# A hybrid backbone layer: raw weight buffers taken in turn, one head's filling, modulation's closing products, and four adds on GpSimd

## The chip, the core and the metric

The kernel runs on one core of a Trainium2 chip. The time is the device time of one execution in microseconds (us); for a kernel it is the median of several runs. TensorE (PE) does the matrix products, VectorE (DVE), ScalarE (ACT) and GpSimd (POOL) the elementwise work, and SyncE (SP) issues all the transfers spoken of here, in one queue, in order: a transfer whose wait isn't over holds back those behind it.

## The reference

One layer (DEPTH = 1) over x (1024 tokens x 1024) with 256 context tokens. Cut to what matters:

```python
mod = silu(c) @ w_mod + b_mod
sh1, sc1, ga1, sh2, sc2, ga2 = split(mod, 6)          # six chunks of 1024
hx = rmsnorm(x, g_mix) * (1 + sc1) + sh1
y = mlstm_mixer(hx, hc, w_in, b_gate, head_gain, w_out)   # 4 heads, two directions
x = x + ga1 * y
hx = rmsnorm(x, g_ffn) * (1 + sc2) + sh2
gate, val = split(hx @ w_up, 2)                       # w_up: 1024 x (2 * 2816)
x = x + ga2 * ((silu(col_conv3(gate) + b_conv) * val) @ w_down)
return rmsnorm(x, g_final)
```

Everything is float32 to the outside. The kernel makes one such product of three products of split numbers (high and low part), so one logical product of a 128x128 block is three PE instructions.

## The kernel before, in words

**The mixer.** It runs head by head. `mlstm(h)` is a generator: first the backward state over ten chunks of 128 tokens, then for each of eight token tiles i `scores(i + 2)` (products s, then the weights on DVE and ACT), `values(i)` (the numerators nm on PE, then dn, ha on DVE and ACT) and `readout(i - 1)` (the transposes yp on PE, which read ha). In the last head `readout` writes yh and yl, the split output, straight to the tiles that the out-projection reads. Each `yield` of `mlstm` carries a number, and `weave(main, fill)` adds these up and runs one unit of the filler for each whole one, and what is left of the filler behind the head. The numbers in the part over the token tiles are multiples of `pace` (1; in the last head 0.8). In heads 0 to 2 the filler is the projections of the next head (pv, pk, pq), in the last head `first_pair`: the out-projection of the first two heads, 16 units of twelve products opa (128x512) behind some loads and splits. What follows the last head, `second_pair`, begins with the products opb, which read the last head's yh and yl.

**Modulation beside it.** `along` runs one unit of `mods` after each unit of the filler in heads 0 to 2. `mods` are four sums one after the other (chunks 3, 4, 2 and 5 of w_mod): `mod_sum` loads eight raw tiles, adds each to ga (L658, `acc`) on DVE, and closes with `use(acc)`: for `mod_cols` eight tiny products mcp (L665, 128x2), for `mod_bcast` two products mbp (L676), which read ga.

**The channel mixer.** 22 tiles of 128 columns, ff, each with seven products in the manner of Strassen (p1 to p7), and each of these twelve PE instructions of 128x512: 84 for an ff. The weights of one ff are two raw tiles of 512 KB, rg (gate) and rv (value). `prep_gate` splits rg into ag (high part on ACT, low part on DVE: the names end in h and l). `prep_rest` makes with four adds on DVE the combinations sa and sb (two buffers for both), splits sb into at and sa into as, and then half of rv into av. p1 and p2 read ag, p6 and p5 read as, p3 and p7 read at, p4 reads av. On the other side stand the split activations ba, bs, bt, bu, made once before ff 0 in four k-tiles (their adds partly on GpSimd, L1016). `gate0` adds e and p2 into gt, `finish_gate` and `finish_value` make e, gt, t; t goes to memory (actd). From ff 11 on `act_sums` reads an earlier actd back (sr), makes sw and writes both (sums). `first(ff)` of ff 0 to 3, and with it p1 and p2, runs ahead of the loop (`pre`).

**Buffers and order.** Raw tiles have two buffers under the tag raw and one under raw2 (`raw_tile`). In the channel mixer rg takes raw, rv always raw2, so that rv of an ff can be loaded when av of the ff before has been split. `pp`, the PSUM tiles of the products, has eight buffers. The order of the instructions on each engine is fixed when the program is built: a scheduler sorts them by their dependences, the buffers and the order in which the code issues them; `tc.issue_after(i)` makes it put an instruction behind another.

Of the kernel before, what the change touches and what calls it, by code (L numbers as in the profile page):

```python
# [12 lines left out]
ALU = mybir.AluOpType  # L13
# [3 lines left out]
P = 128  # L17
# [7 lines left out]
H = 4  # L25
DK = 128
DV = 256
DFF = 2816
# [11 lines left out]
def backbone(ctx, tc, x, c, ctxt, c_ctx, w_mod, b_mod, g_mix, g_ffn, w_in, b_gate,  # L40
             head_gain, w_out, w_up, w_conv, b_conv, w_down, g_final, out):
    nc = tc.nc
    V, S, T, G = nc.vector, nc.scalar, nc.tensor, nc.gpsimd
# [6 lines left out]
    w_up = w_up[0]  # L50
    w_down = w_down[0]
    out = out[0]
# [10 lines left out]
    def wtile(name, dt=F32R, n=1024):  # L63
        return wp.tile([P, WT], dt, tag="w", bufs=8, name=name)[:, :n]

    def raw_tile(name, n=1024, other=False):
        tag, b = ("raw2", 1) if other else ("raw", 2)
        return wp.tile([P, WT], F32, tag=tag, bufs=b, name=name)[:, :n]

    def load_raw(src, name, other=False):  # L70

        r = raw_tile(name, other=other)
        nc.sync.dma_start(out=r if len(src.shape) == 2 else r.rearrange("p (a b) -> p a b", a=src.shape[1]), in_=src)
        return r

    def split(raw, name):

        n = raw.shape[1]
        hi = wtile(name + "h", n=n)
        lo = wtile(name + "l", n=n)  # L80
        S.copy(hi, raw)
        V.tensor_tensor(out=lo, in0=raw, in1=hi.bitcast(F32), op=ALU.subtract)
        return hi, lo
# [6 lines left out]
    def kp(src):  # L90
        return src.rearrange("(k p) n -> p k n", p=P)
# [159 lines left out]
    for i in range(16):  # L251
# [3 lines left out]
                    in1=bmc[:, 0:16].unsqueeze(2).to_broadcast([P, 16, 2]), op=ALU.add)  # L255
    V.scalar_tensor_tensor(out=smod, in0=mts[:, 8:16, :], scalar=1.0,
                           in1=gmix.unsqueeze(2).to_broadcast([P, KT, 2]), op0=ALU.add, op1=ALU.mult)
# [230 lines left out]
    def mlstm(h):  # L488
# [69 lines left out]
        def scores(i):  # L558
            ch = i + 2
            jb = NCH + 1 - ch  # L560
            f0, b0 = h * NCH + ch, H * NCH + h * NCH + jb
            sl = slice(i * P, (i + 1) * P)
            sp_ = st(f"s{h}_{i}")
            T.matmul(sp_[:, :P], kT[:, ch * P:(ch + 1) * P], qT[:, sl], start=True, stop=True)
            if i < LCH - 1:
                ktrans(ch, sp_, P)
                kscale(0, ch, sp_, P)

            ee = hp.tile([P, 2, P], F32, tag="ee", bufs=2, name=f"ee{h}_{i}")
            wi = hp.tile([P, 2, P], F32, tag="wi", bufs=3, name=f"wi{h}_{i}")  # L570
            if i % 2 == 0:
                mrows(i // 2)
            for d, (cc, pos) in enumerate(((f0, i), (b0, jb - 2))):
                mrow_ = mb[d, pos // 2][:, pos % 2, :]
                V.scalar_tensor_tensor(out=ee[:, d, :], in0=mrow_, scalar=uco[:, cc:cc + 1],
                                       in1=zmask[:, d, :], op0=ALU.subtract, op1=ALU.max)
                S.activation(out=wi[:, d, :], in_=mrow_, func=AF.Exp, scale=-1.0,  # L577
                             bias=mpco[:, cc:cc + 1])
            S.activation(out=ee, in_=ee, func=AF.Exp, scale=-1.0)
            V.tensor_tensor(out=ee, in0=ee, in1=sp_[:, :P].unsqueeze(1).to_broadcast([P, 2, P]), op=ALU.mult)  # L580
            wh = hp.tile([P, 2, P], F32R, tag="wh", bufs=3, name=f"wh{h}_{i}")
            wl = hp.tile([P, 2, P], F32R, tag="wl", bufs=3, name=f"wl{h}_{i}")
            S.copy(wh, ee)
            V.tensor_tensor(out=wl, in0=ee, in1=wh.bitcast(F32), op=ALU.subtract)
            V.tensor_tensor(out=wi, in0=wi, in1=qT[:, sl].unsqueeze(1).to_broadcast([P, 2, P]), op=ALU.mult)
            ws[i] = wh, wl, wi, f0, b0, jb
# [27 lines left out]
        def readout(i):  # L614
            sl = slice(i * P, (i + 1) * P)
            ha = hs.pop(i)
            yp = st(f"yp{h}_{i}")
            for f in range(2):
                T.transpose(yp[:, f * P:(f + 1) * P], ha[:, f * P:(f + 1) * P], ident)
            if h < H - 1:  # L620
                yt = hp.tile([P, 2, P], F32, tag="yt", bufs=2, name=f"yt{h}_{i}")
                for f in range(2):
                    S.mul(yt[:, f, :], yp[:, f * P:(f + 1) * P], hgain[:, 2 * h + f:2 * h + f + 1])
                nc.sync.dma_start(out=ydram[h][:, :, sl].rearrange("f p t -> p f t"), in_=yt)
            else:
                for f in range(2):
                    yh, yl = yhl[h][f]
                    gcol = hgain[:, 2 * h + f:2 * h + f + 1]
                    S.mul(yh[:, sl], yp[:, f * P:(f + 1) * P], gcol)
                    V.scalar_tensor_tensor(out=yl[:, sl], in0=yp[:, f * P:(f + 1) * P], scalar=gcol,  # L630
                                           in1=yh[:, sl].bitcast(F32), op0=ALU.mult, op1=ALU.subtract)

        pace = 1 if h < H - 1 else 0.8
        scores(0)
        yield pace
        scores(1)
# [8 lines left out]
        yield pace  # L645
        readout(LCH - 1)

    def mod_sum(chunk, name, use, acc):

        V.memset(acc, 0.0)  # L650
        nc.sync.dma_start(out=acc[0:1, :], in_=b_mod[:, chunk * D:(chunk + 1) * D])
        for k in range(KT):
            r_ = load_raw(w_mod[k * P:(k + 1) * P, chunk * D:(chunk + 1) * D], f"{name}r{k}", True)
            yield
            yield
            dve = next(i for i in reversed(nc.cur_bb.bb.instructions) if i.engine == mybir.EngineType.DVE)
            with tc.issue_after(dve):
                V.scalar_tensor_tensor(out=acc, in0=r_, scalar=sct[:, k, 0:1], in1=acc, op0=ALU.mult, op1=ALU.add)  # L658
        use(acc)

    def mod_cols(dst, gain=None):
        def use(acc):
# [53 lines left out]
    def along(units, side):  # L716

        for i, _ in enumerate(units):
            if i > 2:
                next(side, None)  # L720
            yield

    mods = chain(mod_sum(3, "m3", mod_cols(h2col), ga2), mod_sum(4, "m4", mod_cols(s2col, gffn), ga2),
                 mod_sum(2, "m2", mod_bcast(ga1), ga1), mod_sum(5, "m5", mod_bcast(ga2), ga2))
    EARLY = 6
    late = iter(())
# [127 lines left out]
    def split_to(hi, lo, src):  # L854
        S.copy(hi, src)
        V.tensor_tensor(out=lo, in0=src, in1=hi.bitcast(F32), op=ALU.subtract)
# [12 lines left out]
        trans2(0, tt - 4)  # L869
        split_to(ba[tt - 4][0], ba[tt - 4][1], bs[0, tt - 4])  # L870

    def add(out_, a_, b_, op=ALU.add):
        V.tensor_tensor(out=out_, in0=a_, in1=b_, op=op)  # L873

    def b_op(i, kt):

# [6 lines left out]

    aw = {}

    def load_up(ff, off, name, other=False):
        return load_raw(kp(w_up[:, off + ff * P:off + (ff + 1) * P]), f"{name}{ff}", other)

    def prep_gate(ff, raw=None):

        h_, l_ = split(raw if raw is not None else load_up(ff, 0, "rg"), f"ag{ff}")
        aw[ff, 1] = h_[:, :512], l_[:, :512]
        aw[ff, 2] = h_[:, 512:], l_[:, 512:]
# [16 lines left out]
    second_pair(range(4), 1, norm2)  # L910
    second_pair(range(4, 8), 0, first_half)
    rg0 = load_up(0, 0, "rg")
    prep_gate(0, rg0)
    second_pair(range(4, 8), 1, norm2)
# [15 lines left out]
    def split_b(i, kt, src):  # L930
        split_to(*b_op(i, kt), src)

    def prep_rest(ff, rg):

        rv = load_up(ff, DFF, "rv", True)
        sa, sb = [pc.tile([P, 1024], F32, tag="sx", bufs=2, name=f"{n}{ff}") for n in ("sa", "sb")]
        a11, a12, a21, a22 = rg[:, :512], rg[:, 512:], rv[:, :512], rv[:, 512:]
        add(sa[:, :512], a21, a22)
        add(sa[:, 512:], sa[:, :512], a11, ALU.subtract)
        add(sb[:, :512], a11, a21, ALU.subtract)  # L940
        add(sb[:, 512:], a12, sa[:, 512:], ALU.subtract)
        h_, l_ = split(sb, f"at{ff}")
        aw[ff, 7], aw[ff, 3] = (h_[:, :512], l_[:, :512]), (h_[:, 512:], l_[:, 512:])
        yield
        h_, l_ = split(sa, f"as{ff}")
        aw[ff, 5], aw[ff, 6] = (h_[:, :512], l_[:, :512]), (h_[:, 512:], l_[:, 512:])
        yield
        w_ = wtile(f"av{ff}")
        split_to(w_[:, :512], w_[:, 512:], a22)
        aw[ff, 4] = w_[:, :512], w_[:, 512:]  # L950
# [7 lines left out]
    def first(ff, pq=None):  # L958
        p1, p2 = pq or products(ff, (1, 2))
        e1 = u2k(f"e{ff}")  # L960
        S.copy(e1, p1)
        return e1, p2
# [45 lines left out]

    PRE = 4
    rest0 = prep_rest(0, rg0)  # L1010
    next(rest0)
    pre = [first(0), first(1)]
# [24 lines left out]
    def prep_next(ff):  # L1037

        rg = load_up(ff, 0, "rg")
        res = None  # L1040
        if ff >= PRE:
            prep_gate(ff, rg)
            res = first(ff)
        for _ in prep_rest(ff, rg):
            pass
        return res or pre[ff]

# [204 lines left out]
```

## Time and profile before

| | us |
|---|---|
| median of 3 runs | 1230.25 (1229.15 to 1230.99) |
| the profiled execution | 1229.65 |
| its span | 1227.9 |
| PE busy in the span | 1188.6 (97%) |
| DVE busy | 887.0 (72%) |
| ACT busy | 508.0 (41%) |
| GpSimd busy | 58.6 (5%) |

The span is what the profiler recorded of that execution, from the first to the last instruction. A busy time counts the time in which an instruction of the engine runs; PE's products overlap, so one of 0.39 us begins each 0.227 us. "Idle before" is the time in which the engine had nothing running, with the event that ended it. The granted clock of PE is given as a share of full speed.

The mixer ends at 520 us, the out-projection and the second norm to 576, the channel mixer's up part from 576 to 1008 (ff 16 starts at 887), then the down part.

### The profile page before, as it was taken

What the parts mean: (1) busy time and instruction counts of PE and PEld (TensorE: products, weight loads), DVE (VectorE), ACT (ScalarE), POOL (GpSimd) and SP (SyncE); (2) the same over time, 40 slices, a digit from 0 to 9 for tenths busy, and PEclk for the clock granted to TensorE, in tenths of its full rate; (3) what the DMA queues carried; (4) which work ended last, traced back from release to release, by engine and by line L of the source; (5) the groups of instructions that cost most, each with busy time, mean ns of one, the idle gap of its engine ahead of it and who ended that gap; (6) DMA issues with size and microseconds to landing.
All of it is one profiled execution on the core that took longest, in us unless ns stands there. A gap on an engine that the chain in (4) does not pass through costs nothing.

```text
span 1227.9 us, 15991 instructions
## 1 busy us (share of the span) xinstructions
PE 1188.6 (97%) x5811; PEld 978.5 (80%) x5811; DVE 887.0 (72%) x1564; ACT 508.0 (41%) x911; POOL 58.6 (5%) x198
## 2 busy tenths in 40 slices
PE   7999999999999999899999999999999999999996
PEld 1788998888888788787777888888877778888885
DVE  3775664566477558636998877788788877985887
ACT  3853353344355435327543342333333344444452
POOL 0100010001001001002000000000000000000011
PEclk9999999999999999999999999999999999999998
DMA  8622243343244342132233223244444459624523
GB/s 322 215 70 62 85 127 95 95 138 104 65 146 155 124 144 77 31 124 104 69 103 103 86 69 103 85 139 144 165 154 155 165 200 398 229 95 151 177 69 120
DMA packets 121248, 161.45 MB, mean 131 GB/s; under 512 B 8140, under 2 KB 83148, under 8 KB 121168
## 3 DMA queue, kind: packets, MB, share of 16 engines
q1 hardware_dynamic: 121168, 160.42, 38.9%
q8 instruction: 46, 0.75, 0.3%
q14 instruction: 34, 0.28, 0.1%
HBM read 125.75 MB, written 34.64 MB: 131 GB/s over the span
## 4 chain that ended last, share of the span: by engine, by line
PE 31%; DVE 13%; DMA 4%; ACT 3%; issue 2%; POOL 0%; DVEq 0%; POOLq 0%; ACTq 0%
PE p L87 5%; PE p L88 5%; PE p L86 5%; DMA rv<-in_f_w_up_dram 4%; PE pa L87 3%; PE pa L86 3%; PE pa L88 3%; PE pb L88 2%; PE pb L87 2%; PE pb L86 2%; DVE sb L873 1%; DVE gt L873 1%; DVE t L977 1%; DVE t L979 1%; DVE sa L873 1%
## 5 line engine op out<-in xcount | busy, mean ns | idle before, releaser
L873 DVE TENSOR_TENSOR gt<-e,p 128x512 f32<-128x512 f32 x66 | 44.9, 682 | 5.7 <-PE p L88 5.6
L611 DVE SCALAR_TENSOR_TENSOR ha<-ha,hms,so 128x256 f32<-128x256 f32 x32 | 15.5, 485 | 44.1 <-POOL hms L126 44.1
L873 DVE TENSOR_TENSOR e<-e,p 128x512 f32<-128x512 f32 x66 | 45.0, 681 | 1.3 <-PE p L88 0.9
L976 ACT ACTIVATE t<-gt,cols 128x1024 f32<-128x1024 f32 x22 | 27.4, 1245 | 42.8 <-DVE gt L873 42.8
L982 ACT ACTIVATE t<-t 128x1024 f32<-128x1024 f32 x22 | 23.4, 1062 | 48.1 <-DVE t L979 48.1
L977 DVE SCALAR_TENSOR_TENSOR t<-gt,cols,t 128x960 f32<-128x960 f32 x22 | 26.8, 1217 | 19.7 <-ACT t L976 19.7
L341 ACT CAST vh<-pv 128x256 fp32r<-128x256 f32 x30 | 11.1, 371 | 60.1 <-PE pv L88 60.1
L86 PE MATMUL p<-bt,av 128*128 128x512 f32 x88 | 34.2, 389 | 0.0
L87 PE MATMUL p<-bt,av 128*128 128x512 f32 x88 | 34.2, 389 | 0.0
L88 PE MATMUL p<-bt,av 128*128 128x512 f32 x88 | 34.2, 389 | 0.0
L125 POOL TENSOR_SCALAR fms<-fms 128x1 f32<-128x1 f32 x8 | 3.8, 472 | 628.2 <-DVE fms L873 628.2
L86 PE MATMUL nm<-vh,wh 128*128 128x258 f32 x64 | 31.0, 484 | 0.0
L342 DVE TENSOR_TENSOR vl<-pv,vh 128x256 fp32r<-128x256 f32 x30 | 12.7, 423 | 24.9 <-ACT vh L341 24.9
L604 ACT ACTIVATE ha<-nm,dn 128x256 f32<-128x256 f32 x32 | 15.1, 473 | 32.6 <-DVE dn L602 31.2
L577 ACT ACTIVATE wi<-mb,bco 128x128 f32<-128x128 f32 x64 | 22.6, 399 | 12.6 <-PE nm L594 8.0
L979 DVE SCALAR_TENSOR_TENSOR t<-gt,cols,t 128x960 f32<-128x960 f32 x22 | 26.7, 1212 | 0.0
L873 DVE TENSOR_TENSOR sa<-rv 128x512 f32<-128x512 f32 x22 | 15.2, 689 | 15.3 <-DMA rv<-in_f_w_up_dram 15.3
L86 PE MATMUL pk<-hx,wk_0h 128*128 128x512 f32 x64 | 25.3, 395 | 0.0
L88 PE MATMUL pq<-hx,wq_0h 128*128 128x512 f32 x64 | 25.1, 393 | 0.0
L86 PE MATMUL pq<-hx,wq_0h 128*128 128x512 f32 x64 | 25.1, 393 | 0.0
L87 PE MATMUL pk<-hx,wk_0l 128*128 128x512 f32 x64 | 25.0, 391 | 0.0
L88 PE MATMUL pk<-hx,wk_0h 128*128 128x512 f32 x64 | 25.0, 390 | 0.0
(1096 smaller groups left out, 4169.8 us busy)
## 6 DMA issues: line engine op xcount, KB each, us to landing
rg<-in_f_w_up_dram SPq DMA_DIRECT2D x25, 512.0 KB, 3.9
rv<-in_f_w_up_dram SPq DMA_DIRECT2D x22, 512.0 KB, 4.6
actd<-t SPq DMA_DIRECT2D x22, 512.0 KB, 2.8
dr<-in_f_w_down_dram SPq DMA_DIRECT2D x44, 256.0 KB, 5.2
dr<-sums SPq DMA_DIRECT2D x44, 256.0 KB, 2.9
dr<-actd SPq DMA_DIRECT2D x33, 256.0 KB, 5.1
mr<-in_w_mod_dram SPq DMA_DIRECT2D x16, 512.0 KB, 6.6
vor<-in_a_w_in_dram SPq DMA_DIRECT2D x24, 256.0 KB, 4.0
```

The costliest lines, as they stand in the source:

```text
L86: T.matmul(ps, ah, bh, start=first, stop=False)
L87: T.matmul(ps, al, bh, start=False, stop=False)
L88: T.matmul(ps, ah, bl, start=False, stop=last)
L342: V.tensor_tensor(out=vl[:, 0:DV], in0=p_[:, :DV], in1=vh[:, 0:DV].bitcast(F32), op=ALU.subtract)
L577: S.activation(out=wi[:, d, :], in_=mrow_, func=AF.Exp, scale=-1.0, bias=mpco[:, cc:cc + 1])
L604: S.mul(ha, nm[:, 0, :DV], dn[:, 0, :])
L611: V.scalar_tensor_tensor(out=ha, in0=ha, scalar=ms[:, 1:2], in1=so[i], op0=ALU.mult, op1=ALU.mult)
L873: V.tensor_tensor(out=out_, in0=a_, in1=b_, op=op)
L976: S.activation(out=t_, in_=gate, func=AF.Identity, scale=wcv[:, NFF + ff:NFF + ff + 1], bias=bcv[:, ff:ff + 1])
L977: V.scalar_tensor_tensor(out=t_[:, GRID_W:], in0=gate[:, :SEQ - GRID_W], scalar=wcv[:, ff:ff + 1], in1=t_[:, GRID_W:], op0=ALU.mult, op1=A ...
L979: V.scalar_tensor_tensor(out=t_[:, :SEQ - GRID_W], in0=gate[:, GRID_W:], scalar=wcv[:, 2 * NFF + ff:2 * NFF + ff + 1], in1=t_[:, :SEQ - GR ...
L982: S.activation(out=t_, in_=t_, func=AF.Silu)
```

## The change

Four edits, here without the lines that only rename:

```diff
-        pace = 1 if h < H - 1 else 0.8
+        pace = 1 if h < H - 1 else 0.65
...
+    def behind(engine):
+
+        return tc.issue_after(next(i for i in reversed(nc.cur_bb.bb.instructions) if i.engine == engine))
+
     def mod_sum(chunk, name, use, acc):
...
             yield
             yield
-            dve = next(i for i in reversed(nc.cur_bb.bb.instructions) if i.engine == mybir.EngineType.DVE)
-            with tc.issue_after(dve):
+            with behind(mybir.EngineType.DVE):
                 V.scalar_tensor_tensor(out=acc, in0=r_, scalar=sct[:, k, 0:1], in1=acc, op0=ALU.mult, op1=ALU.add)
-        use(acc)
+        yield
+        with behind(mybir.EngineType.PE):
+            use(acc)
...
-    def add(out_, a_, b_, op=ALU.add):
-        V.tensor_tensor(out=out_, in0=a_, in1=b_, op=op)
+    def add(out_, a_, b_, op=ALU.add, eng=V):
+        eng.tensor_tensor(out=out_, in0=a_, in1=b_, op=op)
...
-    def load_up(ff, off, name, other=False):
-        return load_raw(kp(w_up[:, off + ff * P:off + (ff + 1) * P]), f"{name}{ff}", other)
+    turn = iter(range(1000))
+
+    def load_up(ff, off, name):
+        return load_raw(kp(w_up[:, off + ff * P:off + (ff + 1) * P]), f"{name}{ff}", next(turn) % 3 == 2)
...
-    def prep_rest(ff, rg):
-
-        rv = load_up(ff, DFF, "rv", True)
+    def prep_rest(ff, rg, eng=V):
+
+        rv = load_up(ff, DFF, "rv")
...
-        add(sa[:, :512], a21, a22)
-        add(sa[:, 512:], sa[:, :512], a11, ALU.subtract)
-        add(sb[:, :512], a11, a21, ALU.subtract)
-        add(sb[:, 512:], a12, sa[:, 512:], ALU.subtract)
+        add(sa[:, :512], a21, a22, eng=eng)
+        add(sa[:, 512:], sa[:, :512], a11, ALU.subtract, eng)
+        add(sb[:, :512], a11, a21, ALU.subtract, eng)
+        add(sb[:, 512:], a12, sa[:, 512:], ALU.subtract, eng)
...
-        for _ in prep_rest(ff, rg):
+        for _ in prep_rest(ff, rg, G if ff == 1 else V):
```

The third buffer is the old raw2, now taken by every third tile of the channel mixer in the order of the code, rg or rv. The filler's units in the last head fall due more slowly. A modulation sum closes one yield later, and its products are put behind the last PE instruction issued by then: the second mcp moves from inside a run of pk to behind the numerators nm, a decay product and twelve pq, the first one by three products. The four adds of ff 1 go to GpSimd. No product is added or taken away on PE.

On PE, at the end of the last head (yp3_6 and yp3_7 are the readouts of its last two token tiles, opa the filler's products, opb the first products that read yh3 and yl3), before:

```order
L88 MATMUL opa_6_1_5642<-wow1_1l_5368,yh1_1_4794 128x512
L619 MATMUL yp3_6_5656<-ident_68,ha3_6_5576 128x128 x2
L86 MATMUL opa_7_1_5663<-wow0_1h_5360,yh0_0_4677 128x512
...
L88 MATMUL opa_7_1_5663<-wow1_1l_5368,yh1_1_4794 128x512
L619 MATMUL yp3_7_5677<-ident_68,ha3_7_5619 128x128 x2
L86 MATMUL opb_0_0_5733<-wow3_0h_5511,yh3_0_4977 128x512
L87 MATMUL opb_0_0_5733<-wow3_0h_5511,yl3_0_4978 128x512
```

And now:

```order
L619 MATMUL yp3_6_5614<-ident_68,ha3_6_5534 128x128 x2
L86 MATMUL opa_4_1_5621<-wow0_1h_5469,yh0_0_4677 128x512
...
L88 MATMUL opa_4_1_5621<-wow1_1l_5477,yh1_1_4794 128x512
L619 MATMUL yp3_7_5635<-ident_68,ha3_7_5591 128x128 x2
L86 MATMUL opa_5_1_5642<-wow0_1h_5469,yh0_0_4677 128x512
...
L88 MATMUL opa_7_1_5670<-wow1_1l_5477,yh1_1_4794 128x512
L86 MATMUL opb_0_0_5733<-wow3_0h_5546,yh3_0_4977 128x512
```

Three of the filler's units (opa_5 to opa_7, 36 products) have moved from ahead of yp3_7 to between yp3_7 and opb; behind nm_7 and ahead of yp3_7 stand 24 products for 36.

On DVE, at the first ff (names end in the ff: gt0 and e0 are ff 0's, sa1 and sb1 the adds of ff 1), before:

```order
L873 TENSOR_TENSOR gt0_6409<-e0_6202,p2_0_6189 128x512
L873 TENSOR_TENSOR sa1_6428<-rv1_6426 128x512
L873 TENSOR_TENSOR sb1_6429<-rg1_6424,rv1_6426 128x512
L873 TENSOR_TENSOR sa1_6428<-sa1_6428,rg1_6424 128x512
L873 TENSOR_TENSOR sb1_6429<-rg1_6424,sa1_6428 128x512
L82 TENSOR_TENSOR at1l_6435<-sb1_6429,at1h_6434 128x1024
L82 TENSOR_TENSOR as1l_6439<-sa1_6428,as1h_6438 128x1024
L856 TENSOR_TENSOR av1_6442<-rv1_6426,av1_6442 128x512
L873 TENSOR_TENSOR e0_6202<-e0_6202,p6_0_6396 128x512
```

And now, where add's line is L878 and split_to's L861:

```order
L878 TENSOR_TENSOR gt0_6409<-e0_6202,p2_0_6189 128x512
L82 TENSOR_TENSOR at1l_6435<-sb1_6429,at1h_6434 128x1024
L878 TENSOR_TENSOR sa2_6544<-rv2_6542 128x512
L878 TENSOR_TENSOR sa2_6544<-sa2_6544,rg2_6540 128x512
L82 TENSOR_TENSOR as1l_6439<-sa1_6428,as1h_6438 128x1024
L861 TENSOR_TENSOR av1_6442<-rv1_6426,av1_6442 128x512
L878 TENSOR_TENSOR sb2_6545<-rg2_6540,rv2_6542 128x512
L878 TENSOR_TENSOR sb2_6545<-rg2_6540,sa2_6544 128x512
L878 TENSOR_TENSOR e0_6202<-e0_6202,p6_0_6396 128x512
```

The adds of ff 1 have left this place, and those of ff 2 stand in it.

On SP, in the last third of the loop (rv18 and rg19 are raw tiles of ff 18 and 19; sr, sw and sums belong to `act_sums`, with the number ff - 11; actd is t of the ff named), before:

```order
L73 DMA rg19_8826<-in_f_w_up_dram 128x8x128
L1000 DMA sr5_8531<-actd_5732 128x1024
L991 DMA actd_5732<-t16_8520 128x1024
L73 DMA rv18_8717<-in_f_w_up_dram 128x8x128
L1005 DMA sums_6163<-sr5_8531 128x1024
L1006 DMA sums_6163<-sw5_8532 128x1024
```

And now:

```order
L1012 DMA sums_6163<-sr4_8388 128x1024
L1013 DMA sums_6163<-sw4_8389 128x1024
L73 DMA rv18_8717<-in_f_w_up_dram 128x8x128
L1007 DMA sr5_8531<-actd_5732 128x1024
L998 DMA actd_5732<-t16_8520 128x1024
L73 DMA rg19_8826<-in_f_w_up_dram 128x8x128
L1012 DMA sums_6163<-sr5_8531 128x1024
L1013 DMA sums_6163<-sw5_8532 128x1024
L73 DMA rv19_8860<-in_f_w_up_dram 128x8x128
```

The load of rv18 has moved from behind actd of t16 to ahead of it, behind the write of sw4, which belongs to ff 15.

## Rows read from the trace of the kernel before

**Rows 1.** The page, the chain that ended last: by engine, then by line.

```profile
PE 31%; DVE 13%; DMA 4%; ACT 3%; issue 2%; POOL 0%; DVEq 0%; POOLq 0%; ACTq 0%
PE p L87 5%; PE p L88 5%; PE p L86 5%; DMA rv<-in_f_w_up_dram 4%; PE pa L87 3%; PE pa L86 3%; PE pa L88 3%; PE pb L88 2%; PE pb L87 2%; PE pb L86 2%; DVE sb L873 1%; DVE gt L873 1%; DVE t L977 1%; DVE t L979 1%; DVE sa L873 1%
```

**Rows 2.** Stretches: from:to, length, busy of PE, PEld, DVE, ACT, POOL; PEclk, DMA.

```profile
265.00:268.00 3.00, 3.00 (x15) 2.88 (x13) 1.67 (x2) 1.83 (x5) 0.00 (x0) 0.50 0.28 108
610.00:650.00 40.00, 36.26 (x155) 28.27 (x154) 38.01 (x51) 16.36 (x17) 0.00 (x0) 1.00 0.31 99
650.00:850.00 200.00, 200.00 (x883) 165.40 (x882) 158.13 (x210) 67.36 (x73) 0.00 (x0) 1.00 0.32 104
900.00:950.00 50.00, 47.70 (x210) 38.86 (x209) 39.89 (x55) 15.74 (x17) 0.00 (x0) 1.00 0.48 165
950.00:1000.00 50.00, 47.59 (x208) 38.47 (x207) 43.77 (x61) 14.55 (x17) 0.00 (x0) 1.00 0.38 136
```

**Rows 3.** PE's waits: line, what for; us in total, times, longest.

```profile
PE opb L86 <- DVE yl L630: 3.5, 1, 3.5
PE mcp L665 <- DVE ga L658: 2.2, 2, 1.6
PE p L86 <- DVE e L873: 2.0, 1, 2.0
PE h2t L850 <- DVE xn L838: 1.8, 4, 0.6
...
PE mbp L676 <- DVE ga L658: 1.2, 1, 1.2
```

**Rows 4.** PE in time: start, us, instruction, idle before and its end.

```profile
262.84 1.95 PE L665 MATMUL mcp<-ones,ga 128*128 128x2 f32 x16 [1.57 <-DVE ga L658]
...
507.81 0.28 PE L88 MATMUL nm<-vl,wh 128*128 128x258 f32 x1
...
516.39 0.38 PE L619 MATMUL yp<-ident,ha 128*128 128x128 f32 x2
520.29 0.50 PE L86 MATMUL opb<-wow_0h,yh 128*128 128x512 f32 x1 [3.52 <-DVE yl L630]
...
520.87 0.63 PE L88 MATMUL opb<-wow_0l,yh 128*128 128x512 f32 x1
...
523.86 0.57 PE L86 MATMUL opb<-wow_0h,yh 128*128 128x512 f32 x1
```

**Rows 5.** DVE in time, the end of the last head.

```profile
511.97 0.48 DVE L611 SCALAR_TENSOR_TENSOR ha<-ha,hms,so 128x256 f32<-128x256 f32 x1 [1.55 <-POOL hms L126]
...
519.89 0.35 DVE L630 SCALAR_TENSOR_TENSOR yl<-yp,cols,yh 128x128 fp32r<-128x128 f32 x1
```

**Rows 6.** DVE, SP and PE in time, at ff 17 and 18.

```profile
915.34 0.68 DVE L856 TENSOR_TENSOR av<-rv,av 128x512 fp32r<-128x512 f32 x1
...
916.05 0.42 SPq L73 DMA_DIRECT2D rv<-in_f_w_up_dram  x1
...
921.88 0.69 DVE L873 TENSOR_TENSOR sa<-rv 128x512 f32<-128x512 f32 x1 [2.32 <-DMA rv<-in_f_w_up_dram]
...
934.15 0.50 PE L87 MATMUL p<-bt,as18l 128*128 128x512 f32 x1 [1.74 <-DVE as18l L82]
```

**Rows 7.** The tile rv, all its loads: issue to landing.

```profile
DMA to landing us min/median/max: 3.8/4.6/5.8
```

**Rows 8.** GpSimd and DVE in time, ahead of ff 0.

```profile
578.83 1.61 POOL L1016 TENSOR_TENSOR bs<-bs 128x512 f32<-128x512 f32 x1 [0.69 <-DVE bs L873]
...
579.22 1.78 DVE L873 TENSOR_TENSOR sb<-rg,rv 128x512 f32<-128x512 f32 x1
```

**Rows 9.** DVE and PE in time, at ff 0.

```profile
606.40 0.68 DVE L873 TENSOR_TENSOR gt<-e,p 128x512 f32<-128x512 f32 x1
...
609.52 0.39 PE L86 MATMUL p<-bt,av 128*128 128x512 f32 x1
...
613.62 0.68 DVE L873 TENSOR_TENSOR e<-e,p 128x512 f32<-128x512 f32 x1
```

## The prediction

> **What bounds the kernel now.** I read the page's chain first, what ended last: in it PE has 31% of the span, DVE 13%, and the loads of rv alone, out of all transfers, 4% [rows 1]. So the time is PE's own work (busy share in the table above) plus the places where PE stands still; nothing in the change removes a PE product. Second I read the stretches [rows 2]: from 650 to 850 us PE is busy 200.00 of 200.00 us with 883 products, so 200/883 = 0.227 us each at the full clock, and no edit can win there. In 900 to 950 it misses 2.30 us, in 950 to 1000 2.41, in 610 to 650 3.74. Third I read what PE waited for, by line [rows 3]. The waits that the change aims at are opb (3.5), mcp (2.2 in two), mbp (1.2), the products behind e (2.0), and h2t (1.8). Fourth, the granted clock: the row from 265 to 268 us stands at 0.50 of full speed (1.2 GHz instead of 2.4), right behind the second mcp [rows 2]. Behind the opb wait it is the same: there seven products take 523.86 - 520.87 = 2.99 us instead of 7 x 0.227 = 1.59 [rows 4]; some eight products run so, so one such dip costs 8 x 0.20 = 1.6 us, call it 1.7 with the odd product at its edge.
>
> A PE wait costs a little more than its idle time: the first product after it lasts 0.50 (opb) instead of 0.39, and the last one before it is drawn out [rows 4]. I take +0.28 us for each restart (an estimate from the products' 0.39 us end against their 0.227 us pitch, plus 0.11 for the slower first one).
>
> **A: modulation's closing products.** mcp and mbp wait for ga, the sum on DVE, because they are issued right behind it in program order; 2.2 + 1.2 = 3.4 us of idle time [rows 3]. Afterwards `use(acc)` comes one yield later and behind the last PE instruction there: the second mcp goes from inside a run of pk to behind the next nm, decay and twelve pq products (2.7 us of pq alone), the first only three products later (0.7 us against its wait of 0.62, which is the 2.2 less the longest, 1.57) [rows 3, 4]. The idle time goes but for 0.1, and four restarts' worth, say 0.4. The two dips behind mcp are less plain. The products are tiny (128x2, sixteen passes in 1.95 us [rows 4]), and a dip followed both mcp, one after 0.62 us of idle time and one after 1.57. After 2.0 us of plain idle time at 614 no dip shows: the row from 610 to 650 has clock 1.00 [rows 2]. So 1.95 us of tiny products without idle time ahead should do without a dip; I give that 3 in 4 and take 0.75 x 2 x 1.7 = 2.5. A = -(3.3 + 0.4 + 2.5) = -6.2, from -3.3 (both dips stay, no restart gained) to -7.2. The four mod sums end four units later in the weave, which has 72 units for now 69, so nothing is left over.
>
> **B: the last head's pace.** The wait of 3.5 us before opb is for the last of yl: yp_7 was issued at 516.39, and the second half of yl came on DVE at 519.89, behind a split of weights [rows 3 to 5]; nothing was left for PE. At 0.65 three filler units of 12 opa products stay for the end: 36 x 0.227 = 8.2 us stand between yp_7 and opb, twice the chain of 3.9 us (516.39 to 520.29). So 3.52 + 0.28 and the dip of 1.7 go: -5.5. What is taken from inside the head: ahead of yp_7 now stand 24 opa (5.4 us) behind nm_7, where 36 stood; ha_7, which yp_7 reads, ended 4.4 us behind nm_7 (507.81 + 0.28 to 511.97 + 0.48) [rows 4, 5]. It fits by 1 us. The seven earlier steps also lose filler and wait nowhere long now; I take 0 for them, and for the range +3, about 0.4 us a step, half of that last margin. B = -5.5 (-6 to -2.5).
>
> **C: the third raw buffer in the loop.** In the ff from 16 on DVE sets PE's pace: rv18 is issued at 916.05, just when DVE's av17 (915.34) has read the only buffer that rv had, lands after 5.8 us (median of 22: 4.6 [rows 7]), and DVE sat idle 2.32 us for it at 921.88, in order, with gt, t and e queued behind; then as18l comes late for PE at 934.15, which had stood 1.74 us [rows 6]. With three buffers in turn the load no longer waits for av of the ff before, SP issues it about one ff earlier, and the scheduler puts both sa adds of the next ff on DVE before the t of this one. DVE was busy 39.89 and 43.77 of 50 us in these stretches [rows 2], so without the idle time it keeps ahead of PE. PE's 2.30 + 2.41 = 4.7 go, and five restarts of 0.28: C = -6.0 (-4 if a tenth of a load's 4.6 us stays in sight in each ff, to -6.7 with ff 16's wait).
>
> **D: the first ffs, with GpSimd.** The four adds of ff 1 (128x512) leave DVE, where each takes 0.68 and starts 0.60 behind the last. Around them PE stood 2.0 us for e [rows 3], which ended at 614.30 (613.62 + 0.68) [rows 9], and 1.7 us more until 650 (3.74 less 2.04) [rows 2]. What the trace shows of such adds on GpSimd: one takes 1.61 us, and the DVE add that began beside it took 1.78 instead of 0.68 [rows 8]. It is one of four such pairs (DVE 1.33, 1.78, 1.78, 1.61): 6.50 - 2.72 = 3.8 us lost by DVE for four. rv1 is now loaded when GpSimd's adds would run under DVE's bt and bu splits (593 to 606), so DVE loses 3.8 there and gt0, which began at 606.40, ends at 610.9. It holds the PSUM bank that p4_0, begun at 609.52, needs [rows 9]: PE stands 1.4. From gt0 to e DVE's queue then is gt, at1l, two sa2, as1l, av1, two sb2, e: 7 x 0.6 + 2 x 1.15 = 6.5, no shorter than before, since the adds of ff 2 have taken the place of those of ff 1. e ends at 606.4 + 3.8 + 6.6 = 616.8 instead of 614.3: PE loses 2.5 in all, and its second wait of some 3 us is longer than any in rows here without a dip (2.0), so +1.7 at 6 in 10 = +1.0. Against that the 1.7 us behind it (as2, at3, as3) should go with their restarts, -2.4, as sa2 and sb2 are ready an ff earlier. D = +1 (-4 with no loss beside GpSimd, +4).
>
> The Trainium skill, "SBUF — State Buffer", section "Who interferes with whom", says that a DVE instruction with two SBUF inputs contends with a GpSimd instruction that reads SBUF, and that the one issued second is blocked fully. By that rule each add could cost DVE the whole of GpSimd's time and the sum would come out 2.6 later (rival 2); the four pairs agree in kind (DVE is held) and lie below it in size.
>
> **E: h2t.** h2t waited 1.8 us for xn [rows 3], late since ACT stood behind ag2h, whose rg came late; rg2 is now loaded early, into the third buffer. The tail of this wait is norm work that stays. E = -0.7 (0 to -2).
>
> **Sum.** -6.2 - 5.5 - 6.0 + 1.0 - 0.7 = -17.4 against the profiled execution's 1229.65: 1212.2. The median of the runs is 0.6 above that execution, so 1212.8; I round to 1212.5.
>
> **Rivals.**
> 1. The forecast: 1212.5, between 1208 and 1217 by the smaller terms. 0.50.
> 2. The adds on GpSimd hold DVE for their whole length, 4 x 1.6 = 6.4 instead of 3.8: D grows by 2.6, the time is 1215. For it: all DVE work there has two inputs from SBUF. Against: the four pairs. 0.14.
> 3. They hold DVE not at all: e ends at 613.0, PE's wait shrinks by 1.3 and no dip comes: D = -1.3 - 2.4 = -3.7, 1208. Against it the four pairs again. 0.10.
> 4. The last head gives back what opb won: with less filler inside, PE waits for ha and yp in the head. Seven steps of 0.8 us give 5.6, so B is 0: 1218. For it: ha_7 has 1 us to spare. 0.10.
> 5. The third buffer brings nothing in the loop, the change not doing what it says there: rv stands in SP's one queue behind the write of sums, which waits for DVE's sw, and is still not early. C = 0: 1218.5. Against: that write is of the ff before. 0.09.
> 6. Slower. The same queue, worse: rv lands late, and DVE, now with sa(ff+1) queued ahead of this ff's t, e and gt, stalls in order in each of the eleven ffs with sums. By the rows, rv19 would be issued at about 917.7, and PE wants as18l at 932.4 (934.15 less its wait of 1.74 [rows 6]); DVE needs some 3 us from sa19 to as18l, so a landing of up to 11 us costs PE nothing, and beyond that each us costs 11 us in all. It takes 12.6 us to eat the gain, twice the longest of the 22 (5.8) [rows 7]; at 13 the time is 1212.5 + 2 x 11 = 1234.5. 0.07.
>
> **How the numbers follow.** The likeliest is 1, at 1212.5. The range 1205 to 1221 holds cases 1 to 5 with their own spread and leaves out 6 and the ends of 3 to 5, some 0.15. A change of 0.2% (2.5 us) is about what a measurement of this kernel can tell from none. Faster: cases 1 to 5 less the chance that 4 and 5 come together with both dips left, 0.88; same 0.05; slower 0.07.
>
> **What would show it.** A: no idle time ahead of mcp and mbp, clock 1.00 behind both mcp. B: opb starts without a wait, nm waits under 1 us. C: 900 to 1000 us with PE busy 100, no wait of sa for rv's DMA over 0.5. D: GpSimd adds of 1.5 us or more, DVE splits of 1.7 beside them, one PE wait of 3 to 4.5 us ahead of as1, none at as2 and at3. The prediction is wrong if opb's or as18l's wait has moved to another line of like size, if DVE isn't slowed beside GpSimd, or if sa waits longer than before.

## The result, and the profile after

The changed kernel takes 1215.79 us (median of 4 runs, 1215.09 to 1217.93) against 1229.70 beside it: ratio 0.9889, interval 0.9872 to 0.9906, so 13.7 us less. The forecast was 1212.5 in a range of 1205 to 1221: the sign, the range and most of the sum held, and one term, D, was missed by 5 us. Two runs further on, one of e1 (6153 us) and one of e2 (6788 us), lie far outside all others and count in no ratio.

The chain of the page (by engine, by line) is another one now. The loads of rv, 4% of it in [rows 1], are below 1%, and DVE has 1% for 13%:

```profile
PE 49%; DVE 1%; issue 1%; DMA 1%; POOL 1%; ACT 0%; DVEq 0%; POOLq 0%; SPq 0%; ACTq 0%
PE p L86 11%; PE p L87 11%; PE p L88 11%; PE pa L86 3%; PE pa L87 3%; PE pa L88 3%; PE pb L86 2%; PE pb L88 2%; PE pb L87 2%; DMA rg<-in_f_w_up_dram 0%; DMA rv<-in_f_w_up_dram 0%; DVE dr L1179 0%; POOL sb L878 0%; DVE dr L878 0%; POOL fms L126 0%
```

Of the waits of PE in [rows 3], those for mcp, mbp and opb are gone from the list, and so are as16 to as21; the one behind e, 2.0 before, is 8.8 (line, what for; total, times, longest):

```profile
PE p L86 <- DVE e L878: 8.8, 1, 8.8
...
PE h2t L855 <- DVE xn L843: 2.0, 4, 0.8
```

The stretches, as in [rows 2] (busy of PE, PEld, DVE, ACT, POOL, then PEclk): the clock is 1.00 where the closing products stand, PE is full at the end of the last head and from 900 to 1000, and the one bad stretch lies at 605, behind the 8.8 us, with a clock of 0.57:

```profile
100.00:200.00 100.00, 99.98 (x640) 90.46 (x640) 57.05 (x146) 41.64 (x115) 6.98 (x32) 1.00 0.34 100
200.00:300.00 100.00, 100.00 (x552) 86.00 (x552) 63.03 (x153) 42.91 (x117) 7.90 (x36) 1.00 0.38 111
500.00:520.00 20.00, 20.00 (x91) 16.50 (x90) 12.07 (x17) 5.10 (x7) 0.00 (x0) 1.00 0.41 129
605.00:615.00 10.00, 6.88 (x19) 5.52 (x20) 9.13 (x14) 3.23 (x3) 0.00 (x0) 0.57 0.36 105
900.00:950.00 50.00, 50.00 (x222) 41.42 (x221) 44.39 (x62) 15.50 (x18) 0.00 (x0) 1.00 0.45 157
950.00:1000.00 50.00, 50.00 (x223) 41.41 (x222) 40.26 (x54) 18.59 (x21) 0.00 (x0) 1.00 0.57 210
```

When PE reaches the same product in both profiles says where the time went, stage by stage:

| PE's product | before, us | after, us | difference | gained in the stage | forecast |
|---|---|---|---|---|---|
| first nm | 142.94 | 142.01 | -0.9 | -0.9 (start, loads) | 0 |
| last opb | 568.91 | 556.12 | -12.8 | -11.9 | A + B = -11.7 |
| first p | 576.04 | 562.94 | -13.1 | -0.3 | E = -0.7 |
| first as5 | 683.06 | 676.06 | -7.0 | +6.1 | D = +1 |
| first pa | 1008.06 | 994.30 | -13.8 | -6.8 | C = -6.0 |
| the last | 1217.79 | 1203.78 | -14.0 | -0.2 | 0 |

So the question was D. GpSimd in time, the four adds of ff 1:

```profile
584.89 9.66 POOL L878 TENSOR_TENSOR sa<-rv 128x512 f32<-128x512 f32 x1 [11.18 <-DMA rv<-in_f_w_up_dram]
594.51 1.29 POOL L878 TENSOR_TENSOR sb<-rg,rv 128x512 f32<-128x512 f32 x1
...
597.12 1.29 POOL L878 TENSOR_TENSOR sb<-rg,sa 128x512 f32<-128x512 f32 x1
```

and DVE in time beside them:

```profile
583.08 2.49 DVE L861 TENSOR_TENSOR bt<-bs,bt 128x512 fp32r<-128x512 f32 x4
585.48 2.49 DVE L861 TENSOR_TENSOR bu<-bs,bu 128x512 fp32r<-128x512 f32 x4
587.89 0.69 DVE L861 TENSOR_TENSOR av<-rv,av 128x512 fp32r<-128x512 f32 x1
588.49 4.91 DVE L861 TENSOR_TENSOR bt<-bs,bt 128x512 fp32r<-128x512 f32 x8
593.31 0.69 DVE L878 TENSOR_TENSOR gt<-e,p 128x512 f32<-128x512 f32 x1
599.52 1.23 DVE L82 TENSOR_TENSOR at1l<-sb,at1h 128x1024 fp32r<-128x1024 f32 x1 [5.53 <-ACT at1h L81]
602.24 0.69 DVE L878 TENSOR_TENSOR sa<-rv 128x512 f32<-128x512 f32 x1 [1.49 <-DMA rv<-in_f_w_up_dram]
603.74 0.69 DVE L878 TENSOR_TENSOR sa<-sa,rg 128x512 f32<-128x512 f32 x1 [0.81 <-DMA rg<-in_f_w_up_dram]
...
607.29 0.69 DVE L878 TENSOR_TENSOR e<-e,p 128x512 f32<-128x512 f32 x1
```

The forecast had DVE held by GpSimd, as in [rows 8]. It was the other way (e1 to e4 test this): DVE's splits ran at their 0.60 us each, gt0 came no later (13.24 us behind the bs adds that began at 580.07; before 606.40 - 593.16 = 13.24), and GpSimd's first add lasted 9.66 us, until DVE's run of splits ended and gt0 began. All else in the stage follows: the last add ended at 598.41, at1l waited 5.53, rv2 was issued at 598.44 only, since its buffer waits for these adds, and DVE, in order, waited 1.49 and 0.81 more for loads ahead of e. From gt0 (593.31) to the end of e (607.98) DVE took 14.7 us, and 7.8 of them are these three waits.

### The profile page after: what moved, and what is told of

It reads as the page before. It is cut to its first block, busy times and chain, and to the rows that moved or that the text cites. A ratio compares the mean times of both kernels' runs of the same rounds, so it can differ in the third digit from the quotient of the medians.

```text
span 1213.9 us, 16060 instructions
## 1 busy us (share of the span) xinstructions
PE 1182.2 (97%) x5811; PEld 977.6 (81%) x5811; DVE 882.8 (73%) x1560; ACT 508.9 (42%) x911; POOL 71.5 (6%) x202
## 4 chain that ended last, share of the span: by engine, by line
PE 49%; DVE 1%; issue 1%; DMA 1%; POOL 1%; ACT 0%; DVEq 0%; POOLq 0%; SPq 0%; ACTq 0%
PE p L86 11%; PE p L87 11%; PE p L88 11%; PE pa L86 3%; PE pa L87 3%; PE pa L88 3%; PE pb L86 2%; PE pb L88 2%; PE pb L87 2%; DMA rg<-in_f_w_up_dram 0%; DMA rv<-in_f_w_up_dram 0%; DVE dr L1179 0%; POOL sb L878 0%; DVE dr L878 0%; POOL fms L126 0%
## 5 line engine op out<-in xcount | busy, mean ns | idle before, releaser
L878 DVE TENSOR_TENSOR e<-e,p 128x512 f32<-128x512 f32 x66 | 45.1, 684 | 7.6 <-PE p L88 7.4
L878 DVE TENSOR_TENSOR gt<-e,p 128x512 f32<-128x512 f32 x66 | 45.0, 684 | 4.8 <-PE p L88 4.7
L878 DVE TENSOR_TENSOR sa<-rv 128x512 f32<-128x512 f32 x21 | 14.5, 689 | 19.4 <-DMA rv<-in_f_w_up_dram 19.4
L512 ACT ACTIVATE kh<-kt,cco 128x128 fp32r<-128x128 f32 x44 | 15.8, 367 | 23.7 <-PE kt L505 15.4
L86 PE MATMUL pk<-hx,wk_0h 128*128 128x512 f32 x64 | 25.3, 396 | 0.0
```

The source lines that it names most:

```text
L86: T.matmul(ps, ah, bh, start=first, stop=False)
L512: S.mul(kh, tp[:, c0:c0 + P], wc)
L878: eng.tensor_tensor(out=out_, in0=a_, in1=b_, op=op)
```

## Experiments

What the eight kernels are to tell: was the first add held by DVE's run of splits (e1, e3, e4), or is an add on GpSimd slow for another reason (e2), what is each other edit worth alone (e5 to e7), and what does an earlier e bring (e8). The kernel before took 1228.73 beside e1 to e4 and 1229.77 beside the last four (medians).

### e1: the adds back on DVE

```diff
-        for _ in prep_rest(ff, rg, G if ff == 1 else V):
+        for _ in prep_rest(ff, rg):
```

> The changed kernel with the four adds of ff 1 back on DVE, all else as changed. Theory (GpSimd's first add, 9.66 us, was held by DVE's unbroken run of two-input splits, and all that followed it came late): the wait ahead of as1 falls from 8.8 us to about 2.0 and the dip behind it (2.5 us) goes, so 1215.8 - 6.8 - 2.5 = 1206.5, or up to 1209 if waits at as2 and at3 come back. Rival (the loads of rv2 and rg in the shared buffers make e late, not the adds): the wait stays above 5 us and the time above 1211.

Measured: 1208.67, ratio 0.9839 (0.9812 to 0.9865). The wait for e is back at its old length, and no dip follows (PE's wait, then the stretch behind it):

```profile
PE p L86 <- DVE e L878: 2.0, 1, 2.0
```

```profile
605.00:615.00 10.00, 10.00 (x46) 8.28 (x45) 9.93 (x14) 5.99 (x6) 0.00 (x0) 1.00 0.31 107
```

From the first p to as5 this kernel gains 1.8 us on the one before (0.7 of the old waits stay at at3l), where the change lost 6.1. The theory's number was 1206.5 to 1209. The loads share the buffers as in the changed kernel, so the rival, loads alone, falls. Against the changed kernel this is 7.1 us less by the medians and 6.1 by the two ratios, each against the kernel before beside it.

### e2: the adds on GpSimd in the kernel before

```diff
-        for _ in prep_rest(ff, rg):
+        for _ in prep_rest(ff, rg, G if ff == 1 else V):
```

> The kernel before with only the four adds of ff 1 on GpSimd; rv1 then lands at about 606 us, when DVE's run of splits is over. Theory (held by DVE's run): no add over 2 us, the four take 5.2 to 6.4 where DVE took 2.4, e comes 3 to 4 us later, a dip follows; 1229.7 + 3.5 + 2 = about 1235, from 1232. Rival 1 (an add on GpSimd that follows a load is slow wherever it stands): the first takes over 8 us again, the time is above 1239. Rival 2 (the price of my prediction): DVE's instructions beside them take 1.78 instead of 0.68.

Measured: 1239.41, ratio 1.0093 (1.0068 to 1.0119). GpSimd in time:

```profile
605.62 2.17 POOL L873 TENSOR_TENSOR sa<-rv 128x512 f32<-128x512 f32 x1 [19.20 <-DMA rv<-in_f_w_up_dram]
...
610.37 1.29 POOL L873 TENSOR_TENSOR sb<-rg,sa 128x512 f32<-128x512 f32 x1
```

Here rv1 landed 0.9 us before DVE's run ended (gt0 at 606.55). The first add took 2.17 us, a little over the 2 of the theory, and the others 1.29, so rival 1's slow add falls, although the time is above its 1239. DVE beside the later three had nothing to do, so rival 2 isn't seen either. The time is 4 us worse than the theory's 1235: its mechanism held (the wait for e 3.9 instead of 2.0, and a clock of 0.83 from 610 to 620 us), but it left out what comes behind. rv2 was issued right behind av1 (615.04), whose reading frees the single buffer, at 615.76, 2.0 later than before, and PE waited again, for as3 (that this follows from the late load is read from the order and not tested):

```profile
PE p L86 <- DVE e L873: 3.9, 1, 3.9
...
PE p L86 <- ACT as3h L81: 3.0, 1, 3.0
```

### e3: gaps in DVE's run

```diff
+    gap_ = pc.tile([P, 128], F32, name="gap_")
+    def gap(k):
+        if k % 2:
+            with behind(mybir.EngineType.DVE):
+                V.memset(gap_, 0.0)
...
         split_b(7, kt, bs[1, kt][:, 0, :])
+        gap(kt)
...
         split_b(6, kt, bs[1, kt][:, 1, :])
+        gap(kt)
...
         split_b(4, kt, bs[0, kt][:, 1, :])
+        gap(kt)
```

> The changed kernel with six small writes on DVE (128x128, no input) put between the splits that GpSimd's first add stood beside. Theory (held by an unbroken run of instructions with two SBUF inputs): the first add ends within 2 us of the first such write behind its start, the PE wait of 8.8 us falls to 4 to 6, the time to 1210 to 1213. Rival (the add is slow for another reason, or waits until DVE stands still): still over 8 us, time 1215 to 1217.

Measured: 1210.47, ratio 0.9856 (0.9829 to 0.9883). GpSimd, then DVE in time:

```profile
588.62 3.24 POOL L878 TENSOR_TENSOR sa<-rv 128x512 f32<-128x512 f32 x1 [10.97 <-DMA rv<-in_f_w_up_dram]
591.82 1.74 POOL L878 TENSOR_TENSOR sb<-rg,rv 128x512 f32<-128x512 f32 x1
593.52 1.74 POOL L878 TENSOR_TENSOR sa<-sa,rg 128x512 f32<-128x512 f32 x1
595.34 1.62 POOL L878 TENSOR_TENSOR sb<-rg,sa 128x512 f32<-128x512 f32 x1
```

```profile
589.43 1.28 DVE L861 TENSOR_TENSOR bu<-bs,bu 128x512 fp32r<-128x512 f32 x2
590.69 0.17 DVE L939 MEMSET gap__6163<- 128x128 f32 x1
590.77 3.34 DVE L861 TENSOR_TENSOR bu<-bs,bu 128x512 fp32r<-128x512 f32 x2
...
594.18 1.63 DVE L861 TENSOR_TENSOR av<-rv,av 128x512 fp32r<-128x512 f32 x1
595.73 2.38 DVE L861 TENSOR_TENSOR bt<-bs,bt 128x512 fp32r<-128x512 f32 x2
```

A write of 0.17 us was enough. The first add, held since 588.62, ended 1.17 us behind its start (591.86 against 590.69). From then on the two engines took turns, one instruction each, and both waited: GpSimd's next adds took 1.74, 1.74 and 1.62 us for 1.29, and on DVE a pair of splits took 3.34 instead of 1.28, av 1.63 instead of 0.68, another pair 2.38 instead of 1.22. That is 2.06 + 0.95 + 1.16 = 4.2 us lost by DVE for four adds, and the 3.8 of the forecast's D was of this case. PE's wait of 8.8 for e is gone; in its place stands one of 2.2 for gt0, where D had put 1.4:

```profile
PE p L86 <- DVE gt L878: 2.2, 1, 2.2
```

The theory had 4 to 6 us left of this wait, so it was too careful there; its time (1210 to 1213) holds. With the same four adds on GpSimd the kernel ends 5.3 us below the changed one by the medians, 4.1 by the ratios, and its rival (over 8 us, 1215 to 1217) falls.

### e4: a write and a read on GpSimd beside the run

To the kernel of e1, two GpSimd instructions whose results nobody uses, and a small copy on ACT that sets when the first can start:

```diff
         split_b(7, kt, bs[1, kt][:, 0, :])
+    with behind(mybir.EngineType.Activation):
+        S.copy(scr[:, :64], bs[1, KH - 1][:, 0, :64])
+    G.memset(scr, 0.0)
...
+        if ff == 1:
+            G.tensor_copy(scr, a21)
```

> The kernel of e1_adds_on_dve with two extra GpSimd instructions of 128x512 beside DVE's run of splits: first one that only writes, then one that reads rv1 and writes. Theory (DVE's second input holds GpSimd's reads): the write takes under 1.5 us, the read is held until gt0, 6 to 9 us; PE doesn't wait for either, so the time is that of e1 within 1.5 us. Rival (any GpSimd instruction is held): the write takes over 3 us too. Rival (only two-input GpSimd instructions are): the read takes under 2 us.

Measured: 1209.58 in one run, 0.9 above e1. GpSimd, and DVE's end of the run:

```profile
580.86 0.53 POOL L1043 MEMSET scr<- 128x512 f32 x1 [6.40 <-ACT scr L1042]
585.71 8.90 POOL L948 COPY scr<-rv 128x512 f32<-128x512 f32 x1 [4.33 <-DMA rv<-in_f_w_up_dram]
```

```profile
589.24 4.90 DVE L861 TENSOR_TENSOR bt<-bs,bt 128x512 fp32r<-128x512 f32 x8
594.06 0.68 DVE L878 TENSOR_TENSOR gt<-e,p 128x512 f32<-128x512 f32 x1
```

The write ran in 0.53 us beside DVE's adds; the read, with one input only, was held 8.90 us, until 594.61, half a microsecond into gt0, which has one input in PSUM. Both rivals fall: it is GpSimd's reading that DVE's two-input instructions hold, not GpSimd as such, and not its two-input instructions alone. The Trainium skill, "SBUF — State Buffer", section "Who interferes with whom", states this much; that the hold goes on through fourteen instructions of DVE (585.63 to 594.06) is in this trace.

### e5: the three raw buffers alone

```diff
+    turn = iter(range(1000))
-    def load_up(ff, off, name, other=False):
-        return load_raw(kp(w_up[:, off + ff * P:off + (ff + 1) * P]), f"{name}{ff}", other)
+    def load_up(ff, off, name):
+        return load_raw(kp(w_up[:, off + ff * P:off + (ff + 1) * P]), f"{name}{ff}", next(turn) % 3 == 2)
...
-        rv = load_up(ff, DFF, "rv", True)
+        rv = load_up(ff, DFF, "rv")
```

> The kernel before with only the three raw buffers in turn. By the two traces the waits of ff 16 to 21 were worth 6.9 us, and e1_adds_on_dve shows 1.8 us more in the first ffs where the adds stay on DVE: 8.7 less, 1220.5 to 1221.5; no wait of PE for as16 to as21. Rival (the buffers only work together with the other edits): above 1225.

Measured: 1222.51, ratio 0.9934 (0.9905 to 0.9964), so 8.1 less (4.4 to 11.7), with the 8.7 of the theory inside the interval and the median 1 us above its 1221.5. No wait for as16 to as21 is left in its profile, and PE is full:

```profile
900.00:950.00 50.00, 50.00 (x222) 41.39 (x222) 44.13 (x61) 18.46 (x21) 0.00 (x0) 1.00 0.42 148
```

### e6: modulation's closing products alone

```diff
-        use(acc)
+        yield
+        with behind(mybir.EngineType.PE):
+            use(acc)
```

> The kernel before with only modulation's closing products later. My step A said 6.2 less, with the two dips gone 7.1 (3.4 idle, 0.4 restarts, 2 x 1.7): 1222 to 1223.5, clock 1.00 from 100 to 300 us. Rival (the tiny products themselves bring the dip): 3.4 to 3.8 less, 1225.5, clock 0.98 in those stretches.

Measured: 1220.95, ratio 0.9931 (0.9905 to 0.9956), 8.5 less (5.4 to 11.7). Behind both mcp the clock is full, so the tiny products alone bring no dip, and that rival falls (stretches around the two):

```profile
185.00:200.00 15.00, 15.00 (x83) 12.77 (x82) 6.67 (x18) 4.98 (x16) 1.67 (x6) 1.00 0.26 86
260.00:275.00 15.00, 15.00 (x87) 13.09 (x86) 8.70 (x26) 7.12 (x22) 1.73 (x8) 1.00 0.36 105
```

### e7: the pace alone

```diff
-        pace = 1 if h < H - 1 else 0.8
+        pace = 1 if h < H - 1 else 0.65
```

> The kernel before with only the pace of 0.65. My step B said 5.5 less: opb's wait and its restart 3.8, the dip 1.7; 1223.5 to 1225. Rival (the head gives it back in waits of nm and yp): less than 3 us, above 1226.

Measured: 1226.07, ratio 0.9968 (0.9955 to 0.9982), 3.9 less (2.2 to 5.5): between theory (5.5 less) and rival (less than 3), with the median at the rival's 1226. No wait for opb and no dip behind it, but nm waits 1.0 us in three places now (0.6 in two before). The mixer of this kernel up to the last head is that of the kernel before, and yet its mcp waited longer:

```profile
PE mcp L665 <- DVE ga L658: 2.7, 2, 2.1
...
PE nm L594 <- DVE ha L605: 1.0, 3, 0.5
```

### e8: e ahead of av

To the kernel of e1:

```diff
         if ff == 0:
...
+            add(e1, e1, p6)
             nxt = prep_next(1)
```

(with the same add left out of `finish_gate` for ff 0).

> The kernel of e1_adds_on_dve with ff 0's add of e and p6 issued ahead of ff 1's preparation, so that on DVE it stands ahead of av1, 0.6 us earlier. PE's wait ahead of as1 falls from 2.0 to 1.4, the time by 0.6 or not measurably, 1208. Rival (as1l, not e, is what PE waits for): the wait stays at 2.0.

Measured: 1208.84, ratio 0.9829 (0.9805 to 0.9854). The wait is 1.4, as said, so the rival falls, and the time is that of e1 to what can be measured; a wait of 0.6 for as2h has come in its place:

```profile
PE p L86 <- DVE e L878: 1.4, 1, 1.4
...
PE p L86 <- ACT as2h L81: 0.6, 1, 0.6
```

So e1 and e8 are the fastest, some 7 us below the changed kernel by the medians, by taking its fourth edit back; e3, which keeps that edit, lies between. The three other edits add up: 8.1 + 8.5 + 3.9 = 20.5 us alone, and e1, which has all three, is 19.8 below the kernel before by its ratio.

## Why the prediction held, step by step, and where it didn't

By its own signs the prediction was wrong in two places: DVE wasn't slowed beside GpSimd, and sa waits longer for rv than before. The time still lay in the range, since A and B together, and C, came out within 1 us of their terms and the range was 16 us wide. That 1215.79 is rival 2's 1215 is luck: that rival had DVE held longer still.

**A** held: 6.2 forecast, 8.5 (5.4 to 11.7) alone, an interval that holds the forecast. Both dips went, where I had given each 3 in 4. And the wait that went was not always the 2.2 us of [rows 3]: with the same code up to there, the two mcp waited 2.2 in the profile of before, 2.7 in e7, 3.3 in e5 and 3.6 in e2. The price read from that one execution was the lowest of the four.

**B** held with its wait and its dip: 5.5 forecast, 3.9 (2.2 to 5.5) alone. What I set to 0 with a range of +3, the head's own waits, took some back: nm 1.0 for 0.6, and a restart. The rest of the 1.6 isn't found, and the interval reaches to the 5.5. A and B together were 11.9 against 11.7.

**C** held in size (6.8 for 6.0), and one step of its reasoning didn't: I had DVE's wait for rv go. Between 850 and 1000 us DVE waits for rv longer than before, 12.9 us for 10.4 (first before, then after):

```profile
DVE sa L873 <- DMA rv<-in_f_w_up_dram: 10.4, 7, 2.3
```

```profile
DVE sa L878 <- DMA rv<-in_f_w_up_dram: 12.9, 6, 3.4
```

What went is PE's wait behind it. The wait of sa19 now comes an ff ahead of its use (SP and DVE in time):

```profile
911.26 0.38 SPq L73 DMA_DIRECT2D rv<-in_f_w_up_dram  x1
...
916.95 0.69 DVE L878 TENSOR_TENSOR sa<-rv 128x512 f32<-128x512 f32 x1 [3.36 <-DMA rv<-in_f_w_up_dram]
...
918.76 1.22 DVE L82 TENSOR_TENSOR as18l<-sa,as18h 128x1024 fp32r<-128x1024 f32 x1
```

as18l is done at 919.98, and PE asks for it at 923.8: 3.8 us to spare where it was 1.74 late [rows 6]. The load itself left earlier against its use, as forecast: rv19 at 911.26, 31.6 us before PE asks for as19l (942.85), where rv18 had left 16.4 before [rows 6]. But sa19 moved forward too, and the load stands behind the last sb of ff 18 (910.50), whose reading frees its buffer. I had issued it behind the sums, at 917.7 on the old clock; on the new one these were written at 907.73, and it came 3.5 us later. Rival 6 was thus nearer than I had it: 3.8 us of spare, where a landing of up to 11 less a load of 4.6 to 5.8 had left 5 to 6.

**D** is the step that failed: "DVE loses 3.8 there and gt0 ends at 610.9". From [rows 8] I took who waits (DVE) along with how long. GpSimd had waited there too: its add of 578.83, which takes 1.29 us alone, took 1.61, since it came 0.2 us into a DVE add with two inputs, and it got in right behind that one:

```profile
578.61 0.68 DVE L873 TENSOR_TENSOR sa<-rv 128x512 f32<-128x512 f32 x1
```

In the change GpSimd came upon a run of fourteen such instructions and waited for the end of all of them; e1 takes the adds away and the 6.1 with them, e3 breaks the run and gives back the case of the forecast, at 1210.5, and e4 shows what of GpSimd is held. Why GpSimd got in behind one instruction there and only behind the fourteenth here stays open: it isn't that DVE's instructions came without a break, for in the changed kernel itself a GpSimd add got in between two of them 13 us earlier (held by a split that began at 571.34, and then holding the next, whose four take 3.59 for 2.5):

```profile
571.56 2.15 POOL L1023 TENSOR_TENSOR bs<-bs 128x512 f32<-128x512 f32 x1 [0.69 <-DVE bs L878]
572.48 3.59 DVE L861 TENSOR_TENSOR bu<-bs,bu 128x512 fp32r<-128x512 f32 x4
```

The wait of PE had been put at some 4.5 in all (2.0 as before and 2.5 more), and was 8.8; the dip came, as feared at 6 in 10. The waits for as2 and at3 did go. D came out at +6.1, beyond its own range of -4 to +4. Rival 2 had the wrong engine waiting; rival 3 had DVE not held, which came true, but saw no price in it on GpSimd's side. One reading in D was off as well: from gt0 to the end of e DVE had taken 7.9 us (606.40 to 614.30), so a queue of 6.5 is not "no shorter than before".

**E** failed in a small way: h2t waits 2.0 for 1.8, though the stage is 0.3 shorter. rg2 did come early, and ACT made ag2h at 550.88, 3 us ahead of the norm's first xn, where it had stood directly ahead of it before (566.02); so the wait didn't hang on that load.

## What to carry to other kernels

Before an add goes to GpSimd, read what DVE has queued at that time and not only how long such an add takes: beside a long run of two-input instructions it may end only when the run ends, as the changed kernel and e4 show, and every load whose buffer it frees comes late with it. A wait of DVE for a load costs nothing if the work behind it is wanted an iteration later; in a rotation of buffers the gain can be where the wait stands, and not that it is shorter. A wait of PE just ahead of a drop of its clock counts more than its length, and the same wait can differ by a microsecond or more from one execution to the next.

## What the runs showed of the hardware

- One GpSimd instruction (128x512, float32, reading SBUF) lasted 9.66 us in the changed kernel, beside fourteen successive DVE instructions with two SBUF inputs; with DVE out of the way such an add took 1.29. A copy with one input lasted 8.90 beside the same run in e4. The Trainium skill, "SBUF — State Buffer", section "Summary: rules for kernel authors", says that the second one to issue blocks until the first finishes. By that, an estimate of the price is at most one DVE instruction (0.6 us). That is what GpSimd's add of [rows 8] paid (0.3), and not what these two paid: the measurement decides, and the same two engines showed both cases within one kernel.
- Such a wait ended at a DVE write of 0.17 us without inputs (e3), and at gt0, with one input in PSUM (the changed kernel and e4). Once GpSimd was in, DVE and GpSimd took turns (e3).
- The 1.95 us of tiny mcp products are followed by a clock of 1.00 when products stand directly ahead of them (e6). In the kernel before the clock fell to half behind the second one, with 1.57 us of idle time ahead [rows 2, 4]. But the idle time ahead doesn't settle it: behind the first one, with 0.6 us ahead in each of four executions of the same code, the stretch from 185 to 200 us shows 0.89 in the kernel before and in e5, 0.77 in e7, and no drop in e2 (first e7, then e2):

```profile
185.00:200.00 15.00, 14.38 (x63) 12.13 (x62) 6.31 (x17) 4.24 (x13) 0.94 (x4) 0.77 0.29 93
185.00:200.00 15.00, 14.37 (x79) 12.14 (x78) 7.68 (x16) 4.50 (x15) 1.68 (x6) 1.00 0.23 69
```
